# A convolution with residual on one core: when the stores join the transfer queue, and the last residual pair in one load

## The chip, the cores and the metric

The kernel runs on one core of a Trainium2 chip. The metric is the time on the device in microseconds (us). The kernel before takes 122.33 us, the median of three runs (122.24 to 122.38). One more run was taken with the hardware profiler; the span that it covers is 120.6 us. All times inside the kernel are counted from the start of this span.

Five engines work side by side, each with its own instruction queue: TensorE (PE) multiplies matrices, VectorE (DVE) adds the residual, ScalarE (ACT) packs the input, GpSimd (POOL) clears the constants, and SyncE (SP) issues nearly all transfers. The transfers themselves are carried out by 16 DMA engines. The engines tell each other of progress by semaphores, which are counters.

## The reference

Sixteen images of 64 channels and 64 x 64 pixels go through a 3 x 3 convolution with padding 1 to 64 channels, and a residual of the output's shape is added. All is float32.

```python
def setup_inputs():
    batch, c_in, h, w, c_out, k = 16, 64, 64, 64, 64, 3
    # x, residual: 16 x 64 x 64 x 64; weight: 64 x 64 x 3 x 3

def reference(x, weight, residual):
    pad = k // 2
    x_pad = np.pad(x, ((0, 0), (0, 0), (pad, pad), (pad, pad)), mode='constant')
    ...
                for kh in range(k):
                    for kw in range(k):
                        output[b, co] += weight[co, ci, kh, kw] * x_pad[b, ci, kh:kh+h, kw:kw+w]
    return (output + residual).astype(np.float32)
```

The input, the residual and the output are 16.78 MB each, the weights 0.15 MB.

## The kernel before

Two images make a pair, whose 2 x 64 channels fill the 128 partitions, so there are eight pairs. The tile `ro` holds the whole residual; VectorE adds the convolution into it in place, and the stores read the result from it. Three buffers `xr` take the input, pair by pair.

The residual comes in seven loads, listed in `RES` with the pairs, the pixels and the input load behind which each one is queued. The last pair comes in two halves:

```python
    EARLY = (slice(0, 2), slice(2, 4), slice(4, 6), slice(6, 7))
    WHOLE, LEFT, RIGHT = slice(0, NPIX), slice(0, NPIX // 2), slice(NPIX // 2, NPIX)
    RES = (
        (slice(0, 1), WHOLE, None),
        (slice(1, 2), WHOLE, 1),
        (slice(2, 4), WHOLE, 3),
        (slice(4, 6), WHOLE, 5),
        (slice(6, 7), WHOLE, 7),
        (slice(7, 8), LEFT, 7),
        (slice(7, 8), RIGHT, 7),
    )
    NR = 3
```

Three semaphores `s_r` take turns for these loads. A load waits until the one that had its semaphore before has landed:

```python
    def load_ro(i, e):
        pairs, cols, _ = RES[i]
        if i >= NR:
            e.wait_ge(s_r[i % NR], 16 * (i // NR))
        return e.dma_start(out=ro[:, pairs, cols], in_=res_bc[:, pairs, cols]).then_inc(s_r[i % NR], 16)

    def wait_ro(e, i):
        e.wait_ge(s_r[i % NR], 16 * (i // NR + 1))
```

SyncE's program is a list of loads, then a wait, then the stores of pairs 0 to 6, each group released by a count of VectorE's adds:

```python
        for p in range(NPAIR):
            if p >= NXR:
                nc.sync.wait_ge(s_half, 2 * (p - NXR) + 3)
            ...                                  # load_x(p); the weights behind p == 0
            for i, (_, _, behind) in enumerate(RES):
                if behind == p:
                    load_ro(i, nc.sync)

        wait_ro(nc.sync, len(RES) - 2)           # the left half of the last pair has landed
        for pairs in EARLY:
            nc.sync.wait_ge(s_add, 2 * pairs.stop + 1)
            store(pairs).then_inc(s_out, 16)
```

VectorE handles image n in two adds, the even and the odd rows (`par`). The first of them waits until TensorE has finished the image:

```python
        for n in range(B):
            ...                                  # at a new pair: wait for its residual
            for par in range(2):
                i = nc.vector.tensor_tensor(
                    out=o4[hp, :, par, :], in0=psj[64 * par : 64 * par + 64, :, :], in1=o4[hp, :, par, :], op=ADD
                )
                if par == 0:
                    i._wait_ge(s_conv, n + 1)

                i.then_inc(s_add if par == 0 or n == B - 1 else s_bank, 1)
```

The last pair is stored at the very end, in two halves, when VectorE has done its last add:

```python
    for cols in (LEFT, RIGHT):
        store(slice(NPAIR - 1, NPAIR), cols)
```

The semaphore `s_id` counts preparations. GpSimd's memsets bring it to `NZERO` = 12, and one increment each of TensorE, ScalarE and VectorE, all for the weights, bring it to `NZERO + 3`. Nothing else counts it in this kernel.

Of the kernel before, what the change touches and what calls it, by code (L numbers as in the profile page):

```python
# [15 lines left out]
def kernel(  # L16
# [7 lines left out]
    nc = tc.nc  # L24
# [13 lines left out]
    NZERO = 4 + 2 * NXP  # L38
# [5 lines that stand above are left out]
        (slice(2, 4), WHOLE, 3),  # L44
        (slice(4, 6), WHOLE, 5),
        (slice(6, 7), WHOLE, 7),
        (slice(7, 8), LEFT, 7),
        (slice(7, 8), RIGHT, 7),
    )
    NR = 3  # L50

    res_bc = residual.rearrange("(p b) c h w -> (b c) p (h w)", b=2)
# [18 lines left out]
    s_x = [sem(f"s_x{i}") for i in range(NXR)]  # L71
    s_r = [sem(f"s_r{i}") for i in range(NR)]
    s_out = sem("s_out")
    s_id = sem("s_id")
# [6 lines left out]
    def load_x(p):  # L81
        return nc.sync.dma_start(out=xr[p % NXR][:, :], in_=x_bc[128 * p : 128 * p + 128, :]).then_inc(s_x[p % NXR], 16)
# [10 lines that stand above are left out]
    def store(pairs, cols=slice(0, NPIX)):  # L93
        return nc.sync.dma_start(out=out_bc[:, pairs, cols], in_=ro[:, pairs, cols])
# [21 lines left out]
    def to_the_front(dma):  # L116

        def fixed(ap):  # L120
            t = ap.bass_ap.tensor.name
            return mybir.PhysicalAccessPattern(
                ap=ap.ap, offset=ap.bass_ap.offset, dtype=ap.dtype, memref=t, memsetref=t + "_set", bass_ap=ap.bass_ap
            )

        front = nc.main_func.blocks[0].instructions
        here = nc.cur_bb.bb.instructions
        ins = here.pop()
        assert ins.name == dma.ins.name
        at = next(i for i, e in enumerate(front) if e.engine == ins.engine)  # L130
        front.insert(at, copy.replace(ins, ins=[fixed(a) for a in ins.ins], outs=[fixed(a) for a in ins.outs]))
# [5 lines left out]
    def weight_block(h, half, d, par, kh):  # L137

        at = 64 * half + 32 * h
        return dict(out=wl[at : at + 32, d, :, par, :], in_=tp[0:32, kh, 0:384].rearrange("p (kw co h) -> p kw co h", kw=3, h=2)[:, :, :, h])  # L140

    with tc.tile_critical(no_gpsimd_drain=True):  # L142
# [5 lines that stand above are left out]
            if p == 0:  # L148
                to_the_front(load_x(p))
                nc.sync.dma_start(out=wraw[:, :], in_=w_rows[:, :]).then_inc(s_w, 16)  # L150
            else:
                load_x(p)
            for i, (_, _, behind) in enumerate(RES):
                if behind == p:
                    load_ro(i, nc.sync)

        wait_ro(nc.sync, len(RES) - 2)
        for pairs in EARLY:
            nc.sync.wait_ge(s_add, 2 * pairs.stop + 1)
            store(pairs).then_inc(s_out, 16)  # L160


        nc.gpsimd.memset(ident[:, :], 0.0).then_inc(s_id, 1)  # L163
        nc.gpsimd.wait_ge(s_id, 1)
        nc.gpsimd.affine_select(  # L165
            out=ident[:, :],
            in_=ident[:, :],
            compare_op=mybir.AluOpType.not_equal,
            fill=1.0,
            base=0,  # L170
            pattern=[[-1, 128]],
            channel_multiplier=1,
        ).then_inc(s_id, 1)
        nc.gpsimd.wait_ge(s_id, 2)
        for t in xp:
            nc.gpsimd.memset(t[0:64, 0, :], 0.0).then_inc(s_id, 1)  # L176
            nc.gpsimd.memset(t[64:128, J, :], 0.0).then_inc(s_id, 1)  # L177
        nc.gpsimd.memset(wl[0:64, 0, :, 1, :], 0.0).then_inc(s_id, 1)  # L178
        nc.gpsimd.memset(wl[64:128, 1, :, 0, :], 0.0).then_inc(s_id, 1)  # L179


        to_the_front(load_ro(0, nc.scalar))
        for n in range(B):
            p, im = divmod(n, 2)
            hp = slice(64 * im, 64 * im + 64)
            x4 = xr[p % NXR].rearrange("q (j two w) -> q j two w", two=2, w=W)
            t = xp[n % NXP]
            if im == 0:
                nc.scalar.wait_ge(s_x[p % NXR], 16 * (p // NXR + 1))
            i = nc.scalar.copy(out=t[64:128, 0:J, :], in_=x4[hp, :, 0, :])  # L190
            i.then_inc(s_half, 1)
            if n >= NXP:
                i._wait_ge(s_conv, n - NXP + 1)
            nc.scalar.copy(out=t[0:64, 1 : J + 1, :], in_=x4[hp, :, 1, :]).then_inc(s_pack, 1)  # L194
            if n == 0:
                nc.scalar.wait_ge(s_id, NZERO + 1)
                for b in blocks[4:]:
                    for h in range(2):
                        i = nc.scalar.copy(**weight_block(h, *b))  # L199
                i.then_inc(s_id, 1)  # L200


        nc.vector.wait_ge(s_id, NZERO + 1)
        for k, b in enumerate(blocks[:4]):
            for h in range(2):
                i = nc.vector.tensor_copy(**weight_block(h, *b))  # L206
                if k == h == 0:
                    i.then_inc(s_bank, 2)
        i.then_inc(s_id, 1)
        for n in range(B):  # L210
            p, im = divmod(n, 2)
            hp = slice(64 * im, 64 * im + 64)
            o4 = ro[:, p, :].rearrange("q (j two w) -> q j two w", two=2, w=W)
            psj = ps[n % 2].rearrange("q c j w -> q (c j) w")
            if im == 0:
                for i, (pairs, cols, _) in enumerate(RES):
                    if pairs.start <= p < pairs.stop:
                        wait_ro(nc.vector, i)
# [5 lines that stand above are left out]
                    i._wait_ge(s_conv, n + 1)  # L224

                i.then_inc(s_add if par == 0 or n == B - 1 else s_bank, 1)


        nc.tensor.wait_ge(s_id, NZERO)
        nc.tensor.wait_ge(s_w, 16)  # L230
        wraw3 = wraw.rearrange("p (ci t) -> p ci t", t=9)
        for t in range(9):
            i = nc.tensor.transpose(  # L233
                out=tp[0:32, t // 3, 128 * (t % 3) : 128 * (t % 3) + 128], in_=wraw3[:, :, t], identity=ident[:, :]
            )
        i.then_inc(s_id, 1)
        nc.tensor.wait_ge(s_id, NZERO + 3)
        with nc.Fori(0, B // NXP, 1, engines=[PE]):
            for n in range(NXP):
                nc.tensor.wait_ge(s_bank, 1).then_inc(s_bank, -1)  # L240
                nc.tensor.wait_ge(s_pack, 1).then_inc(s_pack, -1)  # L241
                order = [(1, 0), (1, 1), (0, 0), (0, 1), (2, 0), (2, 1)]
                for i, (kw, d) in enumerate(order):
                    xlo, xhi = max(0, 1 - kw), min(W, W + 1 - kw)
                    for c in range(NCHUNK):
                        j0 = JC * c
                        m = matmul(
                            ps[n % 2][:, c, :, xlo:xhi],
                            wl[:, d, kw, :, :].rearrange("q r c -> q (r c)"),
                            xp[n][:, j0 + d : j0 + d + JC, xlo + kw - 1 : xhi + kw - 1],  # L250
                            i == 0,
                            i == len(order) - 1,
                            c == 0,
                        )
                m.then_inc(s_conv, 1)
# [37 lines left out]
```

## Time and profile before

| what | value |
|---|---|
| time, median of three | 122.33 us (122.24 to 122.38) |
| profiled span | 120.6 us |
| TensorE busy | 87.7 us (73%) |
| VectorE busy | 76.0 us (63%) |
| ScalarE busy | 63.1 us (52%) |
| one add of 64 x 2048 elements | 2.288 us, 32 of them |
| bytes read, bytes written | 33.70 MB, 16.78 MB |
| mean rate of the transfers | 419 GB/s |

The prediction shows lines of several views. The slices cut the span into 40 equal parts; a digit is an engine's busy share of a slice in tenths, and the last row gives the rate of the transfers. A line of the waits reads: the engine that waited, the line of the kernel, what it waited for, then the sum in us, how many times, and the longest. A line of the time line reads: start in us, duration in us (of all the instructions that are merged in it), engine, line, operation, tiles, count, and in brackets how long the engine was idle before and what ended this. A small q behind an engine's name means its instruction queue, so SPq is SyncE's. L82 and L88 are the loads of the input and the residual, L94 is the stores, L220 is VectorE's add.

### The profile page before, as it was taken

What the parts mean: (1) busy time and instruction counts of PE and PEld (TensorE: products, weight loads), DVE (VectorE), ACT (ScalarE), POOL (GpSimd) and SP (SyncE); (2) the same over time, 40 slices, a digit from 0 to 9 for tenths busy, and PEclk for the clock granted to TensorE, in tenths of its full rate; (3) what the DMA queues carried; (4) which work ended last, traced back from release to release, by engine and by line L of the source; (5) the groups of instructions that cost most, each with busy time, mean ns of one, the idle gap of its engine ahead of it and who ended that gap; (6) DMA issues with size and microseconds to landing.
All of it is one profiled execution on the core that took longest, in us unless ns stands there. A gap on an engine that the chain in (4) does not pass through costs nothing.

```text
span 120.6 us, 734 instructions
## 1 busy us (share of the span) xinstructions
PE 87.7 (73%) x389; PEld 10.7 (9%) x105; DVE 76.0 (63%) x40; ACT 63.1 (52%) x37; POOL 2.4 (2%) x16
## 2 busy tenths in 40 slices
PE   0000609999999999999999999999999999400000
PEld 0000300111101110101010101010101010000000
DVE  0000080039898898988989898898988989890000
ACT  4001999999988595875959578595800000000000
POOL 5200000000000000000000000000000000000000
PEclk9999999999999999999999999999999999995555
DMA  7999999999999999999999999999999999999994
GB/s 239 429 424 429 430 429 429 429 435 435 435 429 429 424 429 424 429 435 424 435 429 435 435 435 418 421 459 435 429 429 429 429 429 435 435 435 429 399 427 168
DMA packets 3808, 50.48 MB, mean 419 GB/s; under 512 B 352, under 2 KB 480, under 8 KB 480
## 3 DMA queue, kind: packets, MB, share of 16 engines
q1 hardware_dynamic: 3664, 48.38, 94.2%
q10 hardware_dynamic: 144, 2.10, 4.1%
HBM read 33.70 MB, written 16.78 MB: 419 GB/s over the span
## 4 chain that ended last, share of the span: by engine, by line
PE 71%; DVEq 2%; DVE 2%; issue 0%
PE ps L101 54%; PE ps L100 17%; DVEq L142 2%; DVE ro L220 2%
## 5 line engine op out<-in xcount | busy, mean ns | idle before, releaser
L220 DVE TENSOR_TENSOR ro<-ps,ro 64x2048 f32<-64x2048 f32 x32 | 73.2, 2288 | 17.7 <-PE ps L101 17.2
L101 PE MATMUL ps<-xp,wl 128*128 128x504 bf16 (+1 forms) x288 | 80.0, 388 | 0.2
L190 ACT CAST xp<-xr 64x2048 bf16<-64x2048 f32 x16 | 30.3, 1896 | 22.5 <-PE ps L101 13.1
L100 PE MATMUL ps<-xp,wl 128*128 128x504 bf16 (+1 forms) x92 | 35.9, 390 | 3.4 <-PEq L241 3.4
L194 ACT CAST xp<-xr 64x2048 bf16<-64x2048 f32 x16 | 30.4, 1898 | 0.4
L100 PEld LDWEIGHTS ps<-xp,wl 128*128 128x128 bf16 x96 | 9.5, 99 | 79.1 <-issue 79.1
L206 DVE CAST wl<-ps 32x192 bf16<-32x192 f32 x8 | 2.8, 348 | 14.9 <-PE ps L233 14.8
L233 PE MATMUL ps<-ident,wraw 128*32 128x128 f32 x9 | 2.1, 412 | 12.6 <-DMA wraw<-in_weight_dram 12.6
L233 PEld LDWEIGHTS ps<-ident,wraw 128*32 128x32 f32 x9 | 1.2, 137 | 13.0 <-issue 12.6
L190 ACT ACT_TABLE_LOAD x1 | 1.3, 1283 | 1.1 <-SPq L142 1.1
L199 ACT CAST wl<-ps 32x192 bf16<-32x192 f32 x4 | 1.2, 306 | 0.0
L177 POOL MEMSET xp<- 64x64 bf16 x4 | 0.6, 146 | 0.2
L176 POOL MEMSET xp<- 64x64 bf16 x4 | 0.6, 144 | 0.2
L165 POOL TENSOR_SCALAR_AFFINE_SELECT ident<-ident 128x128 f32<-128x128 f32 x1 | 0.3, 292 | 0.2 <-POOL ident L163 0.2
L179 POOL MEMSET wl<- 64x192 bf16 x1 | 0.3, 253 | 0.1
L178 POOL MEMSET wl<- 64x192 bf16 x1 | 0.3, 251 | 0.1
L163 POOL MEMSET ident<- 128x128 f32 x1 | 0.2, 204 | 0.7 <-SPq L142 0.7
L277 POOL MEMSET const-bfloat16-1.0<- 128x1 bf16 x1 | 0.1, 111 | 0.0
L277 POOL MEMSET const-uint8-127<- 128x1 uint8 x1 | 0.1, 111 | 0.0
L277 POOL MEMSET const-float32-1.0<- 128x1 f32 x1 | 0.1, 108 | 0.0
L277 POOL MEMSET const-float32-0.0<- 128x1 f32 x1 | 0.1, 103 | 0.2 <-issue 0.2
## 6 DMA issues: line engine op xcount, KB each, us to landing
xr<-in_x_dram SPq DMA_DIRECT2D x8, 2048.0 KB, 14.4
out_dram<-ro SPq DMA_DIRECT2D x3, 4096.0 KB, 19.2
ro<-in_residual_dram SPq DMA_DIRECT2D x2, 4096.0 KB, 20.7
ro<-in_residual_dram SPq DMA_DIRECT2D x2, 2048.0 KB, 18.1
ro<-in_residual_dram ACTq DMA_DIRECT2D x1, 2048.0 KB, 12.0
ro<-in_residual_dram SPq DMA_DIRECT2D x2, 1024.0 KB, 18.8
out_dram<-ro SPq DMA_DIRECT2D x1, 2048.0 KB, 13.7
out_dram<-ro SPq DMA_DIRECT2D x2, 1024.0 KB, 9.4
```

Source lines behind the costliest of these rows:

```text
L100: return e.matmul(out=out_, lhsT=lhsT, rhs=rhs, start=start, stop=stop, skip_group_check=True)
L101: return e.add_instruction(mybir.InstMatmult(name=nc.get_next_instruction_name(), engine=PE, ins=[e.lower_ap(rhs), e.lower_ap(lhsT)], outs ...
L142: with tc.tile_critical(no_gpsimd_drain=True):
L176: nc.gpsimd.memset(t[0:64, 0, :], 0.0).then_inc(s_id, 1)
L177: nc.gpsimd.memset(t[64:128, J, :], 0.0).then_inc(s_id, 1)
L190: i = nc.scalar.copy(out=t[64:128, 0:J, :], in_=x4[hp, :, 0, :])
L194: nc.scalar.copy(out=t[0:64, 1 : J + 1, :], in_=x4[hp, :, 1, :]).then_inc(s_pack, 1)
L199: i = nc.scalar.copy(**weight_block(h, *b))
L206: i = nc.vector.tensor_copy(**weight_block(h, *b))
L220: i = nc.vector.tensor_tensor(out=o4[hp, :, par, :], in0=psj[64 * par : 64 * par + 64, :, :], in1=o4[hp, :, par, :], op=ADD)
L233: i = nc.tensor.transpose(out=tp[0:32, t // 3, 128 * (t % 3) : 128 * (t % 3) + 128], in_=wraw3[:, :, t], identity=ident[:, :])
L277: nc = _bacc.Bacc("TRN2", target_bir_lowering=False, num_devices=1)
```

## The change

Two things are changed together. The last residual pair is loaded as a whole, so there are six residual loads in place of seven. And the wait that SyncE makes ahead of the stores is a different one: it no longer waits for the left half of that load to land, but for one more count of `s_id`, which VectorE gives by an instruction of its own, behind the first add of image 12, the thirteenth. By the change's own words SyncE queues the stores when VectorE begins to add that image. The wait decides from when on stores stand in the same queue as loads.

```diff
@@ -44,9 +44,9 @@
         (slice(2, 4), WHOLE, 3),
         (slice(4, 6), WHOLE, 5),
         (slice(6, 7), WHOLE, 7),
-        (slice(7, 8), LEFT, 7),
-        (slice(7, 8), RIGHT, 7),
+        (slice(7, 8), WHOLE, 7),
     )
+    MANY = 12
     NR = 3
 
@@ -154,7 +154,7 @@
-        wait_ro(nc.sync, len(RES) - 2)
+        nc.sync.wait_ge(s_id, NZERO + 4)
         for pairs in EARLY:
             nc.sync.wait_ge(s_add, 2 * pairs.stop + 1)
             store(pairs).then_inc(s_out, 16)
@@ -224,6 +224,8 @@
                 i.then_inc(s_add if par == 0 or n == B - 1 else s_bank, 1)
+                if par == 0 and n == MANY:
+                    nc.vector.sem_inc(s_id, 1)
```

The per-image waits of the stores on `s_add` stay as they were, and so does everything that TensorE and ScalarE do.

## The prediction, made before the changed kernel ran

> **What bounds the kernel now.** I read the slices of the page first, then its DMA queues, then the waits of SyncE's queue, and last the time line around the stores. The slices (40 of 3.015 us each) carry most of the argument:
>
> ```profile
> PE   0000609999999999999999999999999999400000
> DVE  0000080039898898988989898898988989890000
> DMA  7999999999999999999999999999999999999994
> GB/s 239 429 424 429 430 429 429 429 435 435 435 429 429 424 429 424 429 435 424 435 429 435 435 435 418 421 459 435 429 429 429 429 429 435 435 435 429 399 427 168
> HBM read 33.70 MB, written 16.78 MB: 419 GB/s over the span
> ```
>
> The reader is to see that the DMA row has no hole. From slice 1 to slice 38 it stands at 9, and the bytes move at 420 to 435 GB/s; only the first and the last slice are partly empty. TensorE stops in slice 34 and VectorE in slice 35, yet the span runs on to slice 39 with nothing but stores. 50.48 MB at 430 GB/s are 117.4 us of a span of 120.6 us. The page's chain of work (71% PE) ends with VectorE and doesn't tell of this tail; the transfers set the end, not TensorE.
>
> A kernel whose DMA queue is never empty loses exactly the time for which the queue is made empty. So the question is what SyncE's queue waits for, and what the queue holds at that time:
>
> ```profile
> SPq L82 <- ACT xp L190: 53.8, 5, 19.3
> SPq L94 <- DVE ro L220: 21.6, 2, 11.6
> SPq L94 <- DMA ro<-in_residual_dram: 16.6, 1, 16.6
> SPq L88 <- DMA ro<-in_residual_dram: 0.6, 1, 0.6
> ```
>
> The third line is the wait that the change replaces: SyncE waits 16.6 us, once, for the left half of the last residual pair. The time line of SyncE's issues gives the moments:
>
> ```profile
> 59.60 1.90 SPq L88 DMA_DIRECT2D ro<-in_residual_dram  x3
> 78.23 32.30 SPq L94 DMA_DIRECT2D out_dram<-ro  x6
> ```
>
> All loads have been issued by 61.5 us. Asked for the stretches around 60.1 and 61.2 us, the list of DMA issues gives 18.1 us to landing for the left half (60.1 + 18.1 = 78.2, when the stores begin) and 19.5 us for the right half, issued at 61.15. So **the last load lands at 80.65 us**. The first store was issued 2.4 us earlier, so it waits behind that load in the queue and the DMA engines pass from reads to writes without a pause. The last store is issued at 109.3 and takes 10.4 us: it lands at 119.7, and the span ends 0.9 us later. From 80.65 to 119.7 are 39.05 us for 16.78 MB, 430 GB/s: the stores run at the full rate from the last load to the end.
>
> **When the thirteenth image is added.** VectorE's time line:
>
> ```profile
> 83.24 4.61 DVE L220 TENSOR_TENSOR ro<-ps,ro 64x2048 f32<-64x2048 f32 x2 [0.58 <-PE ps L101]
> 88.43 4.61 DVE L220 TENSOR_TENSOR ro<-ps,ro 64x2048 f32<-64x2048 f32 x2 [0.58 <-PE ps L101]
> 93.62 4.61 DVE L220 TENSOR_TENSOR ro<-ps,ro 64x2048 f32<-64x2048 f32 x2 [0.58 <-PE ps L101]
> ```
>
> The first add begins at 26.19 us and each image takes 5.19 us, so image n = 12 begins at 26.19 + 12 x 5.187 = 88.43 us. Its first half takes 2.29 us, to 90.72.
>
> The new increment is not attached to that add: it is a semaphore instruction after it. Whether it fires at the add's start or at its end is worth 2.3 us. The trace has a witness on the same engine:
>
> ```profile
> L142 DVEq DRAIN  x1: 4640/4640/4640, 104.0 to 104.0; - x1
> ```
>
> This drain stands behind the last two adds in program order. The first of them starts at 103.99 and the second ends at 108.6; the drain starts at 104.0. VectorE's sequencer had thus handed both adds over and gone on; only a drain stays until they end. An increment at this place should fire within about 0.1 us of the add's start.
>
> **What the Trainium skill says.** PSUM — Partial Sum Buffer, section "Engine vs sequencer instructions": a semaphore operation of its own is carried out by the sequencer, which waits only until earlier instructions are dispatched, so such an increment can fire while the earlier one is in flight. The drain's start at 104.0 agrees. DMA: Bandwidth & Descriptors, section "Where 436 GB/s comes from", gives 435 GB/s as the ceiling of the path to SBUF; the trace's full slices are at 424 to 435, so they have nothing to spare. The same page, "Anatomy of one DMA", puts a fixed cost of about 2.0 us on each transfer beside its bytes, most of it before completion is told. That fit is for another issuing path (GpSimd's); here the first packets show in the window from 1.00 us, 1.0 us after the first issue at 0.00, and the last bytes move until about 118.95, 0.75 us before the last landing: 1.75 us in all.
>
> **The change part by part.**
>
> 1. *One load instead of two halves.* It removes one issue (about 0.4 us of SyncE) and the 0.6 us wait of that issue for an earlier residual load. Both happen near 61 us, with some 19 us of loads queued. The same 2 MB go at the same place in the queue; the two slices near the halves show 418 and 421 GB/s instead of 430, so at most some 2.5% of 5 us, 0.1 us, may come back. VectorE needs this pair at 98.8 us, long after either landing. Value: 0 to -0.1 us at the landing of the last load, and nothing at the end, since what follows it is now a pause.
>
> 2. *The new wait.* SyncE's first store goes from 78.23 to 88.43 + 0.1 = 88.5 us, 10.3 us later. In front of it the queue runs dry: the last load lands at 80.65 and nothing else is queued.
>
> 3. *What the pause costs.* From 88.5 on the stores are back to back. Pairs 0 to 3 (8.39 MB, 19.5 us) are released at once, pairs 4 and 5 at the end of the half add, 90.72, pair 6 at 101.1, pair 7 at 108.6 + 0.3. At those times the transfers still have bytes to move until about 109, 119 and 124 us, so no later release opens a second hole. The end is 88.5 (issue) + 1.75 (first packet and last landing) + 39.05 (bytes) = **129.3 us**, against 119.7 now: +9.6. Taking the fixed cost from the start of the kernel instead (the first two loads and the weights, 4.34 MB or 10.1 us of bytes, have landed at 12.5 us, so 2.4 us) gives 129.95: +10.2. I choose the middle, leaning to the lower: +9.8. The 0.9 us of closing work stays.
>
> 4. *Compute.* TensorE, ScalarE and VectorE keep their times: their data land before they are needed, in both kernels, and no load depends on a store. A semaphore instruction on VectorE takes 21 ns in the closing part of this trace, beside a 2.29 us add. Value: 0.
>
> Sum: 122.33 + 9.8 = **132.1 us**.
>
> **Rivals.**
>
> - *The increment fires when the add is done* (90.7 instead of 88.5): +12.0, 134.4 us. For it: semaphores attached to an add do behave so in this kernel (pairs 4 and 5 wait for just that). Against: the drain at 104.0, and the increment is an instruction of its own. One in ten.
> - *The wait is hidden*: the end could be set by the last image, whose store can't be issued before 108.9 us; then earlier stores have slack, and the time stays 122.3. With all other stores done, the end would come at 108.9 + 4.9 (2.10 MB) + 1.75 = 115.6. Against: the last landing is at 119.7 already, 4.1 us above that floor, and the DMA row is full to 118; the queued stores are the bound now, and a later start can't be absorbed. Two in a hundred.
> - *Loads and stores apart go faster*: with no mixing the stores could run nearer the ceiling. At 435 GB/s the 16.78 MB need 38.6 us, 0.45 less. The slice of the turn from loads to stores shows 459, not a loss, so mixing costs nothing to win back: 131.6 at best.
> - *The stores delay the last loads now, and whole loads free something upstream*: only 2.4 us of overlap exist, and the right half isn't needed until 98.8 us. Worth nothing.
>
> **Range and chances.** The main reading spans a fixed cost of 1.75 to 2.4 us and 0.45 us of rate, with the spread of the runs (0.14 us): 131.2 to 132.7. Stretched for what I can't see, such as a slower start of a write from an empty queue, 130.9 to 133.4 should hold it eight times in ten; most of the rest is the increment at the add's end. 2% is 2.45 us, so slower by over 2% is nearly sure: 0.97; within 2% 0.02; faster 0.01.
>
> **What would show it.** The DMA row of the changed kernel has a hole of three slices, from about 80 to 89.5 us, and the row before and after it stands at 9. SyncE's longest wait becomes about 27 us (61.3 to 88.5), named as VectorE's. The first store is issued within 0.2 us of the thirteenth image's add; if it is at 90.8, step 2 is wrong. VectorE's adds stay at 88.43 and 103.99; if they move, step 4 is wrong. If the hole is there and the span grows by less than its length, the rate of the stores was mis-sized. No hole at all would mean that the increment fires earlier than the program says, and the whole prediction falls.

## The result and the profile after

The changed kernel takes 131.41 us (median of six runs, 130.78 to 131.90) against 122.35 us before (six runs, 122.24 to 122.48). The ratio is 1.074, with a 95% interval of 1.070 to 1.077: it is slower by 9.06 us. The prediction was 132.1 us, with 130.9 to 133.4 as its range. The profiled run is the slowest of the six.

The slices of the changed kernel's page, 40 of 3.25 us each, with VectorE's row and the two rows of the transfers:

```profile
span 130.0 us, 738 instructions
DVE  0000440098988988989889889898898894000000
DMA  7999999999999999999999995005999999999995
GB/s 242 413 449 419 434 424 434 439 424 434 434 429 439 429 424 439 429 429 444 419 429 449 413 429 232 0 0 242 403 403 484 403 434 454 403 434 454 403 419 227
HBM read 33.70 MB, written 16.78 MB: 388 GB/s over the span
```

The bytes are the same. The row of the transfers, which was without a hole, now has two slices of zero and a half-empty slice on each side of them.

The waits of SyncE's queue (waited for, then us in total, times, longest), and its last load and store issues on the time line:

```profile
SPq L94 <- DVEq L228: 27.9, 1, 27.9
...
59.67 0.91 SPq L88 DMA_DIRECT2D ro<-in_residual_dram  x2
88.55 22.04 SPq L94 DMA_DIRECT2D out_dram<-ro  x6
```

The wait of 16.6 us for a load has become one of 27.9 us for VectorE's queue, and the first store is issued at 88.55 us instead of 78.23. VectorE's adds, its new instruction and its drain at the end show when this was:

```profile
88.49 4.61 DVE L220 TENSOR_TENSOR ro<-ps,ro 64x2048 f32<-64x2048 f32 x2 [0.58 <-PE ps L101]
104.05 4.61 DVE L220 TENSOR_TENSOR ro<-ps,ro 64x2048 f32<-64x2048 f32 x2 [0.58 <-PE ps L101]
...
L228 DVEq EVENT_SEMAPHORE  x1: 21/21/21, 88.5 to 88.5; - x1
```

The thirteenth image's add starts at 88.49, the increment behind it runs at 88.5, and SyncE issues 0.06 us after the add's start. Fine stretches around the two edges of the hole (start:end, then the length, the engines' busy times, TensorE's clock, the share of the DMA engines, GB/s):

```profile
79.60:79.70 0.10, 0.10 (x2) 0.00 (x0) 0.10 (x1) 0.10 (x1) 0.00 (x0) 1.00 1.15 492
79.70:79.80 0.10, 0.10 (x2) 0.00 (x0) 0.10 (x1) 0.10 (x1) 0.00 (x0) 1.00 0.01 0
...
89.20:89.40 0.20, 0.20 (x3) 0.00 (x0) 0.20 (x1) 0.00 (x0) 0.00 (x0) 1.00 0.00 0
89.40:89.50 0.10, 0.10 (x2) 0.00 (x0) 0.10 (x1) 0.00 (x0) 0.00 (x0) 1.00 2.29 983
```

The view counts a packet whole in the stretch in which it starts; hence shares above 1. The last load's last packets start before 79.7 us, and the first store's first packets show from 89.4, some 0.9 us after its issue. From start to start the hole is 9.7 us long. A packet of 16 KB takes 0.61 us (worked out: 80 such packets fill 101.9% of the 16 engines' time from 84 to 87 us in the kernel before), so the engines fall idle one after another between 79.7 and about 80.3 us. This accounts for a span that grows by a little less than 9.7 us, by 9.4 (120.6 to 130.0). In these 9.7 us TensorE is busy all the time and VectorE for 8.5 us.

### The profile page after: what moved, and what is told of

Same layout as the page of the kernel before. It is cut to its first block, busy times and chain, and to the rows that moved or that the text cites. A ratio compares the mean times of both kernels' runs of the same rounds, so it can differ in the third digit from the quotient of the medians.

```text
span 130.0 us, 738 instructions
## 1 busy us (share of the span) xinstructions
PE 87.9 (68%) x393; PEld 10.7 (8%) x105; DVE 76.0 (58%) x40; ACT 63.1 (49%) x37; POOL 2.4 (2%) x16
## 4 chain that ended last, share of the span: by engine, by line
PE 66%; DVEq 2%; DVE 2%; issue 0%
PE ps L101 49%; PE ps L100 17%; DVEq L142 2%; DVE ro L220 2%
## 5 line engine op out<-in xcount | busy, mean ns | idle before, releaser
L101 PE MATMUL ps<-xp,wl 128*128 128x504 bf16 (+1 forms) x288 | 80.0, 388 | 0.0
L100 PE MATMUL ps<-xp,wl 128*128 128x504 bf16 (+1 forms) x96 | 37.4, 389 | 3.4 <-PEq L243 3.4
```

The costliest lines, as they stand in the source:

```text
L100: return e.matmul(out=out_, lhsT=lhsT, rhs=rhs, start=start, stop=stop, skip_group_check=True)
L101: return e.add_instruction(mybir.InstMatmult(name=nc.get_next_instruction_name(), engine=PE, ins=[e.lower_ap(rhs), e.lower_ap(lhsT)], outs ...
```

## The experiments

The theory: the cost is the time for which the transfer queue stands empty, no more, and it hangs on the new wait alone. Rivals: the whole load has a part in it; a late release costs as such, by the backlog behind the last image; the increment fires at another time than it seems to.

### Each half of the change alone

**The whole load without the new wait.** SyncE waits for the load of pair 6.

```diff
-        (slice(7, 8), LEFT, 7),
-        (slice(7, 8), RIGHT, 7),
+        (slice(7, 8), WHOLE, 7),
...
         wait_ro(nc.sync, len(RES) - 2)     # unchanged text; it now names pair 6
```

> The last pair is loaded whole, but SyncE still waits for a load: that of pair 6, which should land near 75.9 us, before it queues the stores. Theory of the hole (the cost is the time for which the transfer queue stands empty, and the size of the load is worth nothing): stores queued near 76 us, no hole, 122.3 us, between 122.0 and 122.6. Rival, the whole load has a part in the loss: above 123 us.

Measured: 122.98 us (122.83 to 123.16), ratio 1.0049 (1.0036 to 1.0062). This is 0.4 us over the range I gave, and so a miss of both readings: above 122.6, but just below the 123 that I gave the rival. The stores were issued at 75.74 us and there is no long hole, so nearly all of the 9 us is not here; but 0.6 to 0.7 us asks for a cause, which is taken up below.

**The new wait with the two halves.**

```diff
-        wait_ro(nc.sync, len(RES) - 2)
+        nc.sync.wait_ge(s_id, NZERO + 4)
...
                 i.then_inc(s_add if par == 0 or n == B - 1 else s_bank, 1)
+                if par == 0 and n == MANY:      # MANY = 12
+                    nc.vector.sem_inc(s_id, 1)
```

> Two halves as before, but the wait for the thirteenth image. Theory of the hole: the whole loss is here, first store at 88.5 us, 131.4 us, between 130.8 and 131.9, with the same scatter between runs as the changed kernel (about 1 us). Rival, the whole load has a part: clearly under 130.8.

Measured: 131.05 us (130.54 to 132.01), ratio 1.0736 (1.0702 to 1.0770), against 1.0739 of the whole change. The wait alone makes the whole loss.

### Moving the release

**One image earlier, two images earlier.** `MANY = 12` becomes 11, then 10, in the changed kernel.

```diff
-    MANY = 12
+    MANY = 11
```

> The changed kernel with the increment one image earlier, at about 83.3 us. Theory of the hole: one image, 5.19 us, is taken off the hole one for one, 131.4 - 5.2 = 126.2 us (125.6 to 126.8). Rival, the late release as such costs (through the backlog of stores that stands behind the last image): the loss goes down by another amount than the shift.

> The changed kernel with the increment at image 10, about 78.1 us, some 1.6 us before the last load's bytes end. Theory of the hole: no hole, 122.3 us (122.0 to 122.7). Rival, a release by VectorE costs more than one by a transfer: above 123.

Measured: 126.08 us (125.91 to 126.66) for 11, ratio 1.0324 (1.0304 to 1.0345); 122.45 us (122.35 to 122.64) for 10, ratio 1.0009 (1.0001 to 1.0017). From 12 to 11 the time falls by 5.33 us for a shift of 5.19, which agrees within the scatter of these runs (1.12 and 0.75 us); from 11 to 10 by only 3.63, since there the hole closes. Released at image 10, the changed kernel is as fast as the kernel before, with the whole load and with VectorE's increment in it. Neither of the two costs anything worth naming in that place.

**At the end of the same add.**

```diff
-        nc.sync.wait_ge(s_id, NZERO + 4)
+        nc.sync.wait_ge(s_add, 13)
...
-                if par == 0 and n == MANY:
-                    nc.vector.sem_inc(s_id, 1)
```

> The changed kernel, but SyncE waits for the count that is attached to the first add of image 12 and comes when this add is done, instead of the increment behind it. Theory of the hole: released 2.3 us later than in the changed kernel, near 90.85 us, 131.4 + 2.3 = 133.7 us (133.0 to 134.3). If the increment of the changed kernel came at the add's end too, no difference: 131.4.

Measured: 133.63 us (133.32 to 134.15), ratio 1.0926 (1.0901 to 1.0952): 2.2 us over the changed kernel, for an add of 2.29 us. The runs of both scatter by about 1 us, so the profile is the better witness. Image 12's adds and the first store's issue in it:

```profile
88.05 4.61 DVE L219 TENSOR_TENSOR ro<-ps,ro 64x2048 f32<-64x2048 f32 x2 [0.58 <-PE ps L100]
...
90.36 19.79 SPq L93 DMA_DIRECT2D out_dram<-ro  x6
```

The first add ends at 88.05 + 2.29 = 90.34, and the store is issued 0.02 us later. An increment attached to the add comes when the add is done; the separate one behind it came at its start.

### Filling the hole, and queueing early

**Pairs 0 and 1 ahead of the wait.** The wait for image 12 stays, but one store of 4.19 MB goes in front of it.

```diff
-        nc.sync.wait_ge(s_id, NZERO + 4)
         for pairs in EARLY:
+            if pairs.start == 2:
+                nc.sync.wait_ge(s_id, NZERO + 4)
             nc.sync.wait_ge(s_add, 2 * pairs.stop + 1)
```

> The changed kernel, with the store of pairs 0 and 1 (4.19 MB, 9.75 us of transfer) queued ahead of the wait for the thirteenth image, the others behind it as in the changed kernel. Theory of the hole: this store lies behind the last load from 61 us on and fills the hole of 79.7 to 89.45 us nearly to the brim, so the time is that of the kernel before, 122.3 to 122.7 us, although SyncE's wait still ends at 88.5. Rival, the late release as such: about 131 us, or at least clearly above 123.

Measured: 123.06 us (123.06 to 123.48), ratio 1.0071 (1.0058 to 1.0085). Of the 9.06 us, 8.3 are gone, although all other stores are still held until VectorE reaches image 12. The transfers of this run and SyncE's wait for VectorE:

```profile
DMA  7999999999999999999999999999999999999994
GB/s 227 433 433 421 434 433 433 433 433 433 433 433 427 422 433 433 433 433 427 427 433 433 433 433 433 384 384 427 433 422 433 433 433 433 433 427 433 400 427 189
...
SPq L94 <- DVEq L229: 18.5, 1, 18.5
```

The long wait is there (a wait of 9.0 us for an earlier add stands ahead of these 18.5), and the hole is not. This rejects the rival of the late release as such. A remainder of 0.7 to 0.8 us stays, outside the range I gave, and the row shows a shallow dip: two slices at 384. The next runs show the same dip by itself.

**No wait at all.** SyncE queues the first stores right behind the last load, with the whole load and with the two halves.

```diff
-        wait_ro(nc.sync, len(RES) - 2)
         for pairs in EARLY:
```

> Last pair loaded whole, and no wait at all ahead of the stores but those on the adds: the first stores go into the queue at 61 us, right behind the last load. Theory of the hole: a fuller queue changes nothing, 122.3 us (122.0 to 122.7). Rival, stores that stand in the queue early take transfer time from the loads or fill the queue: later loads, and 123 us or more.

> The kernel before, with its two half loads, but without SyncE's wait for the left half: the first stores go into the queue at 61 us. It stands beside the run with the whole load and no wait (+0.55 us on before, a short dip of the transfers near 79.3 us at the turn from loads to stores), and beside the run with the whole load released at 78.1 us (+0.1 us, no dip). If stores queued long ahead of the turn make the dip, whatever the load's shape: near 122.9 us, with the dip. If the whole load makes it, together with early stores: 122.3 to 122.5 us and no dip.

> The kernel with the whole load and no wait, run again as the partner of the run with halves and no wait, on the same chip: 122.9 us (122.7 to 123.2), with the dip near 79.3 us.

Measured with the whole load: 122.92 us (122.75 to 123.18), and 123.04 us (122.90 to 123.09) when it was run again; with the halves 122.96 us (122.91 to 123.09), ratio 1.0051 (1.0038 to 1.0065). My range for the first was missed by 0.2 us. The shape of the load makes no difference; the early release makes 0.6 us. The stretch of the turn from loads to stores, 78 to 81 us, in the kernel before:

```profile
78.00:81.00 3.00, 3.00 (x16) 0.29 (x3) 2.91 (x2) 2.92 (x2) 0.00 (x0) 1.00 1.03 437
```

without the wait, with the two halves:

```profile
78.00:81.00 3.00, 3.00 (x16) 0.29 (x3) 2.97 (x2) 2.97 (x2) 0.00 (x0) 1.00 1.02 366
```

with the whole load and the wait for pair 6 (stores issued at 75.74 us):

```profile
78.00:81.00 3.00, 3.00 (x15) 0.30 (x4) 2.75 (x2) 2.76 (x2) 0.00 (x0) 1.00 0.98 339
```

and with the whole load and the release at image 10 (stores issued at 78.14 us):

```profile
78.00:81.00 3.00, 3.00 (x16) 0.29 (x3) 2.89 (x2) 2.90 (x2) 0.00 (x0) 1.00 1.00 426
```

The last two numbers are the share of the DMA engines and GB/s. The engines count as busy in all four, but in the two with an early release fewer bytes pass. Against 437 GB/s, 366 are 0.5 us of transfer in these 3 us (71 x 3 / 430) and 339 are 0.7 us, which is the size of the loss. So the wait of the kernel before has a use: stores released at 78.1 to 78.2 us pass the turn at nearly the full rate, stores released at 75.7 us or at about 60 us don't.

The delay can be placed more closely. The list of issues has the time from issue to landing of the last residual load, the right half, first in the kernel before, where it is issued at 61.15 us, then without the wait, where it is issued at 61.06:

```profile
ro<-in_residual_dram SPq DMA_DIRECT2D x1, 1024.0 KB, 19.5
...
ro<-in_residual_dram SPq DMA_DIRECT2D x1, 1024.0 KB, 20.2
```

It lands at 81.3 us instead of 80.65. The left half lands at 78.1 to 78.2 in both. So what early stores delay is the last load itself, by the 0.6 us that the kernel loses. The same holds with the whole load: it lands at 81.2 us with the wait for pair 6 (60.24 + 21.0) and at 80.6 with the release at image 10 (60.10 + 20.5). Why each byte takes longer there is not settled.

**The last pair stored whole.** This is the run with the whole load and the wait for pair 6, with one store at the end.

```diff
-    for cols in (LEFT, RIGHT):
-        store(slice(NPAIR - 1, NPAIR), cols)
+    store(slice(NPAIR - 1, NPAIR))
```

> Like the run with only the whole load, and the last pair is stored whole too, as one transfer instead of two halves. Theory of the hole: the queue is full until the end in any case, so 122.3 us; at best 0.3 us less, from longer runs of bytes and one issue of 1.2 us less behind the last add, at worst 0.3 us more. Rival, the shape of the last transfers sets the end: a difference of over 0.5 us.

Measured: 123.47 us (123.34 to 123.71), 0.5 us over its partner with two half stores: a miss, since I had allowed 0.3. The span, SyncE's wait for the end of the stores and GpSimd's clearing of the semaphores, in this run:

```profile
span 121.7 us, 736 instructions
...
SPq L286 <- POOLq L258: 12.7, 1, 12.7
...
L260 POOLq EVENT_SEMAPHORE_RANGE_CLEAR  x1: 114/114/114, 120.5 to 120.5; - x1
```

and in its partner with the two half stores:

```profile
span 121.3 us, 737 instructions
...
SPq L287 <- DMA out_dram<-ro: 10.3, 2, 7.9
...
L261 POOLq EVENT_SEMAPHORE_RANGE_CLEAR  x1: 114/114/114, 118.3 to 118.3; - x1
```

The last store lands earlier here, at 120.1 us (issued at 107.7, 12.4 us to landing) against 120.4 (109.4 and 11.0), and yet the span ends later. From the last landing to the end are 1.6 us instead of 0.9. With two halves GpSimd clears the semaphores once the first half has landed, at 118.0, while the second half is still on its way. With one store it can begin only behind the last landing, and SyncE waits for it. So the loss is closing work of this kernel that is no longer hidden, not a slower transfer.

### A hole that VectorE has no part in

In the changed kernel the runs lie 1.1 us apart, in the kernel before 0.24. Two profiles of one and the same wait differ by 1.4 us: the changed kernel (the slowest of its six runs), and the new wait with the two halves (the fastest of its six). First the changed kernel, TensorE's matmuls of the first image and the first add:

```profile
21.96 1.48 PE L101 MATMUL ps<-xp,wl 128*128 128x504 bf16 x3
23.25 0.59 PE L100 MATMUL ps<-xp,wl 128*128 128x504 bf16 x1
26.25 4.61 DVE L220 TENSOR_TENSOR ro<-ps,ro 64x2048 f32<-64x2048 f32 x2 [8.52 <-PE ps L101]
```

Then the new wait with the two halves, with its first store and its span:

```profile
21.26 0.38 PE L101 MATMUL ps<-xp,wl 128*128 128x504 bf16 x1
21.48 0.81 PE L102 MATMUL ps<-xp,wl 128*128 128x504 bf16 x3
24.92 4.61 DVE L221 TENSOR_TENSOR ro<-ps,ro 64x2048 f32<-64x2048 f32 x2 [7.26 <-PE ps L102]
...
87.22 12.97 SPq L95 DMA_DIRECT2D out_dram<-ro  x4
...
span 128.6 us, 739 instructions
```

TensorE starts at a slow pace, a group of three matmuls in 1.48 us instead of 0.81. In one run this ends before 21.3 us, in the other after 23.2. The first add is 1.33 us apart (24.92 and 26.25), the first store is 1.33 us apart (87.22 and 88.55), the span 1.4. From the first add to the first store both take 62.30 us, so the whole difference is there before the first add. The Trainium skill's page TensorE: Matmul & The Clock Gate, Part 1 on the clock gate, says that the warm-up goes by a window that runs freely, so that the moment of the change varies from run to run. That it varies agrees with these two profiles. The size does not: the page gives 500 ns to either side, and here the change of pace lies at least 1.9 us apart. That the slow pace is the clock gate is not shown either: the record of the granted clock stands at 1.00 from 18 to 27 us in both.

If this is what scatters, a hole whose end is set by a transfer shouldn't. The kernel before, with its wait put on the right half:

```diff
-        wait_ro(nc.sync, len(RES) - 2)
+        wait_ro(nc.sync, len(RES) - 1)
```

> The kernel before, but SyncE waits for the right half of the last pair to land, not the left half: the stores are released by a transfer at about 80.65 us, with a short hole. In four profiles with a hole the span ends 41.44 us after the first store's issue; from this the span should be 80.65 + 41.44 = 122.1 us, 123.9 us on the device (123.6 to 124.3). The scatter of the runs tells two readings apart: if it comes from VectorE's release, which moves with the moment at which TensorE leaves its slow pace, the runs here agree within 0.4 us like those of before; if any hole in the transfers scatters, they differ by about 1 us as in the changed kernel.

Measured: 123.93 us, four runs from 123.90 to 123.98, ratio 1.0133 (1.0116 to 1.0150). Its store issue, and its hole in the transfers:

```profile
80.61 28.49 SPq L94 DMA_DIRECT2D out_dram<-ro  x6
...
80.00:81.00 1.00, 1.00 (x7) 0.10 (x1) 1.00 (x1) 0.42 (x1) 0.00 (x0) 1.00 0.00 0
81.00:81.50 0.50, 0.50 (x4) 0.03 (x1) 0.20 (x1) 0.00 (x0) 0.00 (x0) 1.00 0.00 0
81.50:82.00 0.50, 0.50 (x4) 0.07 (x1) 0.21 (x1) 0.22 (x1) 0.00 (x0) 1.00 1.22 524
```

There is a hole, and hardly any scatter: 0.08 us. The time is the one that the other holes foretell. All five profiles with a hole, in one table (times in us):

| kernel | first store issued | span | difference | slowest less fastest run |
|---|---|---|---|---|
| wait for the right half | 80.61 | 122.1 | 41.5 | 0.08 |
| image 11 | 82.56 | 124.0 | 41.4 | 0.75 |
| image 12, two halves | 87.22 | 128.6 | 41.4 | 1.47 |
| the changed kernel | 88.55 | 130.0 | 41.5 | 1.12 |
| image 12, add done | 90.36 | 131.8 | 41.4 | 0.83 |

Once the queue has run dry, the end lies 41.4 to 41.5 us after the first store's issue, wherever that is and whatever released it.

## Why the prediction was right

**The bound** (the transfers, not TensorE): right. With a hole the end follows the first store one for one, while TensorE's and VectorE's work stays where it was. The section of the Trainium skill from which the prediction takes 435 GB/s (DMA: Bandwidth & Descriptors, "Where 436 GB/s comes from") says too that about 358 GB/s of the HBM side bind a transfer between HBM and SBUF. Here one core alone moves 429 GB/s from 82 to 118 us in the kernel before, so the measurement decides.

**Step 1, the whole load**: right in its place. At a release of 78.1 us the change with the whole load costs 0.1 us; without the wait, whole and halves agree within 0.1 us. The gain of up to 0.1 us that I allowed isn't seen.

**Step 2, the new wait**: right. The release was foretold at 88.5 and came at 88.55. That it came so close is partly luck: both profiles caught a run in which the first add was late (26.19 and 26.25 us; the profiles of this case range from 24.7 to 26.4). The drain of the kernel before had shown that VectorE's sequencer goes on while adds are in flight. The Trainium skill's sentence on this (PSUM — Partial Sum Buffer, "Engine vs sequencer instructions") is now seen at the place itself: 21 ns at 88.5, with an add that runs to 90.8; and the attached count, 2.2 us later, is the counterpart.

**Step 3, the cost of the pause**: the mechanism is right, the size 0.7 us too high. In spans I had 120.6 + 9.8 = 130.4; the six spans of the changed kernel have a median of 129.5. Two terms of the sum were mis-sized:

- From the first store's issue to the end I had 1.75 + 39.05 + 0.9 = 41.7, and 0.2 more for the choice of a middle between two fixed costs, 41.9 in all. It is 41.44. The lower of the two would have been the better choice, and still 0.26 too long. Its 1.75 has 1.0 us to the first packets, where 0.9 were measured, and 0.75 us from "the last bytes" at 118.95 to the landing; by the view's count 118.95 is where the last packets start, and they still ran on from there.
- The release stood at 88.5 because the one profile of before had its image 12 there. The median run has it at 129.5 - 41.44 = 88.06 (worked out), 0.44 earlier. In that profile TensorE left its slow pace late. In the kernel before this moment costs nothing, so its runs didn't betray it.

Together this is 0.9 us; 0.2 of it is taken back because the time on the device lies 1.9 us above the span here (131.41 and 129.5) and 1.73 in my sum (122.33 and 120.6).

**Step 4, compute**: right. The last two adds start at 104.05, against 103.99.

**The rivals**: the increment at the add's end would have made 133.6 us; I had said 134.4. The hidden wait falls with the result. The faster stores don't fall by the time alone: that rival had 131.6 at best, and 131.41 was measured. The rate rejects it: 429 GB/s from 92 to 127 us in the changed kernel, and 429 from 82 to 118 in the kernel before. The rival that stores delay the loads was called worth nothing. Between the two kernels of the change it is: the last load lands at 80.65 in both. But a release earlier than that of the kernel before does cost 0.6 us, and it is the last load that it delays.

**What would show it**: I had announced a hole from about 80 to 89.5 us and a wait of about 27 us. They are 79.7 to 89.4, and 27.9. I had also said that a span that grows by less than the hole's length would mean a rate mis-sized for the stores. It grew by 9.4 us for 9.7, but the rate is the same; the 0.3 us lie at the hole's front edge, where packets that have started still run on.

No version here beats the kernel before. The rule of 41.44 says how little is left: stores whose data show just when the last load's last packets have started would be issued at 79.7 - 0.9 = 78.8 us and end at 120.2 at the earliest, against a span of 120.6. That is an estimate from the two profiles and no run shows it; since those packets run on to about 80.3 us, the gain would be less than this 0.4 us.

## What to carry to other kernels

When the row of the transfers is full from end to end, ask of each wait of the issuing queue what is queued behind which transfer when the wait ends: a release that comes after the last queued byte costs about the gap plus the start of a transfer (here 0.9 us to the first data), and one that comes too early may cost a little as well (here 0.6 us). A release tied to a transfer keeps step with the transfers; one tied to an image counts on the compute engines' pace, brings their scatter into the time, and is right only as long as nothing shifts. Filling the gap with work that is already done (here one store of 4.19 MB) is nearly as good as moving the release: it left 0.7 to 0.8 us, the earlier release 0.1.

## What the runs showed that I had not expected

- The scatter of 1.1 us: it comes from the moment at which TensorE leaves its slow pace, which the kernel before hides behind its transfers and the changed kernel doesn't.
- Stores that wait in the queue long before the last load ends cost 0.6 us at the turn (medians of 122.92 to 123.06 in five runs that queue them early and end with two half stores, against 122.3 to 122.5 with a release at 78.1 to 78.2 us). It is not the load's shape. The last load lands 0.6 us later in these runs; why stays open.
- One last store of 2.10 MB in place of two of 1.05 MB lands 0.3 us sooner and makes the kernel end 0.5 us later, since GpSimd's closing work then stands behind the last landing.
